# Two-layer hybrid transformer trunk on one core: local attention ahead of latent attention, with nine input projections in pieces beside it, and a conformer convolution over one gapped row

## The chip, the cores and the metric

The kernel runs on one NeuronCore of a Trainium2 chip as one program. The metric is the device time in microseconds (us) of one execution; a profiled execution gives in addition a span, the time between the first and the last recorded instruction. Engines are named as the profile names them: PE (TensorE) multiplies matrices, DVE (VectorE) and ACT (ScalarE) work on tiles element by element, POOL (GpSimd) does some of that too, and SP issues DMAs. Matmul results land in PSUM, everything else lies in SBUF.

## The reference

Two layers run over 256 context tokens and 512 latent tokens of width 1024, in float32. Each layer adds half a SwiGLU feed-forward, then a mixer, then half another feed-forward, each behind a modulated RMS norm and a gate:

```
h += 1/2 * gate1 * SwiGLU_1(mod(norm(h)))
h += gate2 * W_out[ MLA | short conv | windowed GQA + sink | conformer conv ](W_in mod(norm(h)))
h += 1/2 * gate3 * SwiGLU_2(mod(norm(h)))
```

The mixer's four parts read one input projection `W_in` and write into one output projection `W_out`, 256 channels each:

- MLA, here *latent attention*: queries of rank 192, keys and values of rank 128, four heads of 64 + 32 rotary channels; a latent token sees all 768 tokens, a context token the 256 context tokens.
- short conv: `b * dwconv3(c * x)`, three projections of 256 channels.
- windowed GQA, here *local attention*: four query heads, two key heads of 64 channels; a block of 128 latent tokens sees the neighbouring blocks within 128 positions and the context, with a sink in the softmax.
- conformer conv: a gated linear unit, a depthwise convolution over 31 positions with a bias, a layer norm over channels and SiLU. The sequence and the context are convolved apart, each padded with zeros.

Context tokens need no output in the second layer, so that there every query side works on 512 tokens only. The nine modulation vectors of a layer come from products of a conditioning vector with a large weight matrix (`w_mod`).

## The kernel before

Activations lie transposed, channels on partitions and tokens along the row; `TOK` is 768, `SEQ` 512, `CTX` 256. A row holds the 512 latent tokens and then the 256 context tokens. Each matmul runs in a 32-bit format of reduced precision and is made exact enough by splitting both operands into a high and a low part: `split` rounds a tile on ACT (L140) and takes the remainder on DVE (L141), and `mm3` (L169) issues three products. So each weight block of 128 x 512 costs an ACT and a DVE operation before PE can use it (`unit`), and so does each activation tile.

`mixer` (L630) is a Python function that records one layer's mixer in program order; a scheduler then orders each engine's queue by that order and by priorities (`rise`). It records:

1. The norm and the projections of the conformer pair (`T_CFA`, `T_CFG`), then the 31 taps of the conformer convolution on DVE at a low priority (`P_CONV`), so that its operations fill DVE's spare places. `dw_conv` issues a tap as one operation per segment, one over the latent tokens and one over the context.
2. The other 13 projections, each of 8 weight pieces times 3 products over 512 and 256 columns, into three PSUM tiles of 1024 columns that go round (`self.dbl`): latent KV and Q, the window's queries, keys and values, the short convolution's six. Norms, rotations and the first latent queries stand between them.
3. `Latent` units (12 in layer 0, 8 in layer 1): one head and 256 queries each. A unit has two score tiles; each goes through `reduce_max` on DVE (L877), `Exp` with its sum on ACT (L880), `reciprocal` on DVE, normalisation on POOL (L882); then the probabilities are transposed on PE (L602), split by ACT and DVE, and weigh the values on PE (`weigh`, L772 and L773).
4. `Window` units (12, then 8): one block of 128 queries and two heads each, with two PSUM score tiles, the same chain (L825, L833, L837, L840), and the exact sum with the sink.
5. `out` splits each part's result for the output projection; `conformer_norm` goes through its four steps at units that `CN` names.

The loop over units is software-pipelined: the softmax of unit i, the transposes of unit i-1, the values of unit i-2. At the end of a step `spot` lets a generator advance (`fill`), which multiplies one further block of `w_mod` for a later modulation (L186, PSUM tile `mod_ps`, named pmod in the trace; `po`, named pone, collects the weighed values). So a *mod step* is four matmuls with a DMA of its own; the profile records each of them twice.

PSUM is eight banks of 512 columns: pmod, pone and six that the mixer cuts into tiles by `self.psum`. First these are three tiles of 1024, then, for the attention, two of 1024 (`dbls`) and two of 512 (`sgl`).

## Time and profile before

| | us |
|---|---|
| device time, three runs | 2708.47, 2701.59, 2710.09 (median 2708.47) |
| device time of the profiled execution | 2709.64 |
| its span | 2707.9 |
| PE busy | 2635.7 (97%) |
| DVE busy | 2012.7 (74%) |
| ACT busy | 1115.6 (41%) |
| POOL busy | 65.5 (2%) |
| mean granted clock of TensorE | 0.987 of 2.4 GHz |

The span begins with the first recorded instruction and ends with the last, 1.7 us less than the device time. Busy shares are means over the whole span; layer 0's mixer lies between 578 and 892 us, layer 1's between 2040 and some 2300. Lines of the profile are those of the kernel before; after the change the same operations stand some lines further down.

### The profile page before, as it was taken

The numbers are of one execution on the slowest core, as the hardware profiler recorded it, in microseconds if no ns is written. First come the engines' busy times: TensorE is split into PE (matmuls) and PEld (weight loads), VectorE is DVE, ScalarE is ACT, GpSimd is POOL, SyncE is SP. The second block draws the span as 40 slices with busy tenths as digits, with TensorE's granted clock in tenths as the row PEclk, the third lists the DMA queues.
The fourth block names the chain that finished last, engine by engine and source line by source line (L and its number), as shares of the span: only waits on it lengthen the run. The fifth ranks groups of instructions, "written<-read, shape, count | busy, mean of one in ns | idle before, by whom it ended". The sixth has DMA issues, their size and how long they took to land.

```text
span 2707.9 us, 40719 instructions
## 1 busy us (share of the span) xinstructions
PE 2635.7 (97%) x16021; PEld 2446.8 (90%) x16021; DVE 2012.7 (74%) x3940; ACT 1115.6 (41%) x2098; POOL 65.5 (2%) x88
## 2 busy tenths in 40 slices
PE   7999999999989999999999999999999989999998
PEld 5999999988866999999999999999998866889998
DVE  5777666778777486777667867776678786788887
ACT  4323333342376342333224523343244376544444
POOL 0000000000022000000000000000000022000000
PEclk9999999999989999999999999999999989999999
DMA  7323223221123342323223122221122213323322
GB/s 265 115 89 107 86 85 103 94 93 55 55 79 125 98 135 81 115 80 117 75 92 122 55 94 71 64 78 61 63 84 96 71 63 117 118 86 105 99 94 79
DMA packets 78272, 254.68 MB, mean 94 GB/s; under 512 B 8704, under 2 KB 14336, under 8 KB 77824
## 3 DMA queue, kind: packets, MB, share of 16 engines
q1 hardware_dynamic: 78080, 252.08, 28.7%
q8 instruction: 125, 2.05, 0.3%
q14 instruction: 67, 0.55, 0.1%
HBM read 249.95 MB, written 2.10 MB: 93 GB/s over the span
## 4 chain that ended last, share of the span: by engine, by line
PE 91%; DVE 3%; DMA 3%; ACT 2%; issue 1%; POOL 0%; DVEq 0%; SPq 0%; ACTq 0%; POOLq 0%
PE ps L169 74%; PE pone L169 8%; PE pmod L169 3%; PE pmod L186 3%; PE ps L602 1%; DMA mraw<-in_w_mod 1%; PE pone L772 1%; PE pone L773 1%; DMA raw<-in_w_gu 0%; DMA i<-in_w_mod 0%; DMA h<-in_h 0%; DVE r L141 0%; ACT f L140 0%; PE ps L279 0%; ACT f L833 0%
## 5 line engine op out<-in xcount | busy, mean ns | idle before, releaser
L169 PE MATMUL ps<-x,wh 128*128 128x384 f32 (+1 forms) x3064 | 748.8, 329 | 0.0
L169 PEld LDWEIGHTS ps<-x,wh 128*128 128x128 f32 x3064 | 542.8, 188 | 0.1
L169 PE MATMUL ps<-x,wl 128*128 128x384 f32 (+1 forms) x1532 | 505.2, 330 | 0.2 <-ACT x L297 0.2
L140 ACT ACTIVATE wh<-raw 128x512 fp32r<-128x512 f32 x439 | 274.7, 627 | 463.9 <-PE ps L169 316.4
L169 PE MATMUL ps<-t,wh 128*128 128x384 f32 (+2 forms) x1488 | 385.5, 341 | 0.3 <-DVE t L141 0.3
L141 DVE TENSOR_TENSOR wl<-raw,wh 128x512 fp32r<-128x512 f32 x439 | 301.2, 688 | 104.7 <-ACT wh L140 102.1
L169 PE MATMUL ps<-r,wh 128*128 128x512 f32 (+3 forms) x1362 | 339.5, 351 | 0.2 <-DVE r L298 0.2
L303 DVE SCALAR_TENSOR_TENSOR h<-ps,hg,h 128x256 f32<-128x256 f32 (+3 forms) x404 | 186.8, 506 | 187.2 <-PE ps L169 186.5
L169 PEld LDWEIGHTS ps<-x,wl 128*128 128x128 f32 x1532 | 287.8, 188 | 7.9 <-issue 3.7
L169 PEld LDWEIGHTS ps<-t,wh 128*128 128x128 f32 x1488 | 269.2, 188 | 7.1 <-DVE t L141 0.5
L140 ACT ACTIVATE wh<-t 128x512 fp32r<-128x512 f32 x217 | 136.0, 629 | 336.2 <-PE ps L169 200.2
L169 PEld LDWEIGHTS ps<-r,wh 128*128 128x128 f32 (+1 forms) x1362 | 228.7, 189 | 31.8 <-DVE r L298 1.5
L457 DVE TENSOR_TENSOR t<-t,ps 128x384 f32<-128x384 f32 (+1 forms) x422 | 217.2, 520 | 52.1 <-PE ps L169 49.8
L169 PE MATMUL ps<-t,wl 128*128 128x384 f32 (+2 forms) x744 | 253.2, 341 | 1.0 <-ACT t L140 1.0
L140 ACT ACTIVATE t<-t 128x384 fp32r<-128x384 f32 (+2 forms) x247 | 130.4, 536 | 211.9 <-DVE t L451 102.0
L141 DVE TENSOR_TENSOR wl<-t,wh 128x512 fp32r<-128x512 f32 x217 | 149.1, 689 | 90.5 <-ACT wh L140 90.5
L169 PE MATMUL ps<-r,wl 128*128 128x512 f32 (+4 forms) x681 | 212.0, 352 | 0.8 <-ACT r L297 0.8
L169 PE MATMUL ps<-x,t 128*128 128x384 f32 (+1 forms) x1308 | 204.2, 309 | 0.0
L169 PEld LDWEIGHTS ps<-x,t 128*128 128x128 f32 x1308 | 194.1, 188 | 0.0
L169 PE MATMUL ps<-t,t 128*128 128x384 f32 (+2 forms) x948 | 188.8, 345 | 0.0
L169 PEld LDWEIGHTS ps<-t,t 128*128 128x128 f32 x948 | 165.4, 188 | 10.9 <-issue 1.2
L141 DVE TENSOR_TENSOR t<-t,t 128x384 fp32r<-128x384 f32 (+2 forms) x247 | 137.5, 568 | 25.3 <-ACT t L140 24.8
(229 smaller groups left out, 3772.5 us busy)
## 6 DMA issues: line engine op xcount, KB each, us to landing
raw<-in_w_gu SPq DMA_DIRECT2D x160, 512.0 KB, 3.8
mraw<-in_w_mod SPq DMA_DIRECT2D x128, 512.0 KB, 4.4
raw<-in_w_dn SPq DMA_DIRECT2D x88, 512.0 KB, 3.6
raw<-in_w_in SPq DMA_DIRECT2D x34, 512.0 KB, 3.6
raw<-in_w_out SPq DMA_DIRECT2D x20, 512.0 KB, 3.6
i<-in_w_mod SPq DMA_DIRECT2D x32, 256.0 KB, 6.0
raw<-in_w_gu SPq DMA_DIRECT2D x32, 256.0 KB, 3.4
h<-in_h SPq DMA_DIRECT2D x4, 768.0 KB, 6.7
```

Source lines behind the costliest of these rows:

```text
L140: self.nc.scalar.activation(hi, x, AF.Copy)
L141: self.nc.vector.tensor_tensor(out=lo, in0=x, in1=hi.bitcast(F32), op=ALU.subtract)
L169: self.nc.tensor.matmul(ps[:, c:e], a, b[:, c:e], start=start and i == 0, stop=stop and i == 2)
L186: nc.tensor.matmul(ps[32 * j:32 * j + 32, :256], self.sc[:, k, :], r[:, j * 256:(j + 1) * 256], start=k == 0, stop=k == KD - 1)
L303: nc.vector.scalar_tensor_tensor(out=self.h[:, k, s:e], in0=ps[:, s - a:e - a], scalar=gate[:, k, i:i + 1], in1=self.h[:, k, s:e], op0=ALU ...
L457: eng.tensor_tensor(out=out, in0=p, in1=q, op=op)
L602: self.nc.tensor.transpose(out, in_, self.ident)
L772: nc.tensor.matmul(po[:, :256], v, p[1], start=start, stop=False)
L773: nc.tensor.matmul(po[:, :256], v, p[0], start=False, stop=stop)
```

## The change

The recording order of the mixer is turned round, and four things go with it.

- After the conformer pair only the four window projections are recorded, then `window_operands`. The `Window` units come first. The nine other projections become the generator `others`, which yields after each of its 8 weight pieces; the loop over units takes pieces of it three times per step (`more`), so that they spread evenly over the window stage. They go through `slow`, which accumulates into pmod (512 columns) and a further tile `spare` (256 of 512 columns).
- When the window units are recorded, the latent operands are prepared at once (rotary, queries, keys, values), and the `Latent` units follow. Two mod steps are taken in each of their steps (`fill(2)`), none in the window stage; the output splits and the steps of `conformer_norm` stand at fixed units (j = 4 to 9). The query weights are loaded once per layer.
- PSUM: the transposes keep the two tiles of 512 throughout. The other four banks are two tiles of 1024, then for the window stage one tile `quad` of 1536 columns for both heads of a unit and `spare` of 512, then two tiles of 1024 again. A projection of the first stage may also use the pair of 512.
- The conformer convolution's input row has 15 zeros before, between and behind the segments (written by POOL), so that `gap_conv` runs each tap as one operation over 783 columns (512 + 15 + 256) in layer 0, 512 in layer 1. `conformer_norm` reads the segments from their places.

```diff
 class K:
-    WIN, CN = 2, (2, 4, 0, 1)
+    CN = (4, 6, 8, 9)
+    GAP = CF_K // 2
+    WIDE = TOK + 3 * GAP
...
+    def gap_conv(self, y, u, w, bias, n):
+        nc = self.nc
+        mid = CF_K // 2
+        for j in [mid] + [j for j in range(CF_K) if j != mid]:
+            if j == mid:
+                nc.vector.tensor_scalar(out=y[:, :n], in0=u[:, j:j + n], scalar1=w[:, j:j + 1], scalar2=bias, op0=ALU.mult, op1=ALU.add)
+            else:
+                nc.vector.scalar_tensor_tensor(out=y[:, :n], in0=u[:, j:j + n], scalar=w[:, j:j + 1], in1=y[:, :n], op0=ALU.mult, op1=ALU.add)
...
     def mixer(self, l, n, st):
-        dbls = self.psum(st, 2, 1024)
-        third = st.enter_context(ExitStack())
-        self.dbl = dbls + self.psum(third, 1, 1024)
-        sgl = deque()
+        sgl = self.psum(st, 2, 512)
+        cuts = st.enter_context(ExitStack())
+        self.dbl = self.psum(cuts, 2, 1024)
...
             def softmax(w):
...
                 for g in range(2):
-                    ps = self.turn(dbls)
...
-                    nc.vector.reduce_max(mx[:, g:g + 1], ps[:, c0:TOK], axis=AX.X, negate=True)
-                    pss.append(ps)
+                src = [quad[:, c:c + wide] for c in w.c0]
+                for g in range(2):
+                    nc.vector.reduce_max(mx[:, g:g + 1], src[g], axis=AX.X, negate=True)
...
-        units = [Latent(h, tp) for h in range(4) for tp in range(nq // 2)]
-        units += [Window(t, kv) for kv in range(2) for t in range(nq)]
...
+        def slow(t, nt, m=P):
+            rw = self.load(win[l, t], 1024)
+            w = [self.unit(rw[:, :512]), self.unit(rw[:, 512:])]
+            parts = [(0, SEQ, self.mod_ps)] + ([(SEQ, nt, spare)] if nt > SEQ else [])
+            for k in range(KD):
+                wh, wl = w[k // 4]
+                c = slice((k % 4) * P, (k % 4) * P + m)
+                for a, b, ps in parts:
+                    self.mm3(ps[:m, :b - a], (wh[:, c], wl[:, c]), (x[k][0][:, a:b], x[k][1][:, a:b]), k == 0, k == KD - 1)
+                yield
+            return parts
...
+        units = [Window(t, kv) for kv in range(2) for t in range(nq)]
+        units += [Latent(h, tp) for h in range(4) for tp in range(nq // 2)]
+        nw, per = 2 * nq, nq // 2
+        window_operands()
+        while self.open:
+            self.fill()
+        cuts.close()
+        quad, spare = self.psum(cuts, 1, 1536)[0], self.psum(cuts, 1, 512)[0]
...
         for i in range(len(units) + lv):
+            j = i - nw
+            if j == 0:
+                more(1)
...
+                qw, kw = query_weights(), kv_weights()
+                cuts.close()
+                self.dbl = self.psum(cuts, 2, 1024)
+                mraw = self.mraw
+                self.mraw = deque(mraw + deque([self.raw[2], self.raw[3]]))
+                mla_rotary(*qw)
+                mla_queries(0, *qw)
+                mla_keys(0, kw)
...
+                mla_values(kw)
...
-            self.spot()
+            if j >= 0:
+                self.fill(2)
...
-    N_R, N_F = 27, 14
+    N_R, N_F, N_WIDE = 26, 11, 4
```

Two places show how the engines' queues change. The first is PE at a Window unit of layer 0. Its scores (L819, L822, L824 before; L818, L821, L826 after) go into the tiles ps; L172 is `mm3` after the change, r its x operand, wh and wl the weights. Before, a unit's scores stood like this:

```order
L186 MATMUL pmod<-mraw_65,sc 32x256 x3
L819 MATMUL ps_5064<-r_5020,r_5032 128x384
L819 MATMUL ps_5064<-r_5052,r_5032 128x384
L822 MATMUL ps_5064<-masks_r,ident_r 128x128 x2
L824 MATMUL ps_5064<-r_5020,r_5032 128x256
L824 MATMUL ps_5064<-r_5052,r_5032 128x256
L819 MATMUL ps_5060<-r_5020,r_5036 128x384
L819 MATMUL ps_5060<-r_5052,r_5036 128x384
L822 MATMUL ps_5060<-masks_r,ident_r 128x128 x2
...
L186 MATMUL pmod<-mraw_66,sc 32x256
L602 MATMUL ps_6296<-ident,f_4900 128x128
L772 MATMUL pone<-f_4883,r_5056 128x256
```

After the change the like place reads:

```order
L172 MATMUL pmod<-r_4980,wh_73 128x512
L818 MATMUL ps_5705<-r_5036,r_5020 128x384
...
L821 MATMUL ps_5705<-masks_r,ident_r 128x128 x2
L826 MATMUL ps_5705<-r_5036,r_5020 128x256
...
L826 MATMUL ps_5705<-r_5036,r_5024 128x256
...
L818 MATMUL ps_5705<-r_5036,r_5024 128x384
...
L172 MATMUL ps_5709<-r_4980,wl_74 128x256
L172 MATMUL ps_5709<-r_4984,wh_73 128x256
...
L769 MATMUL pone<-f_4879,r_5052 128x256
...
L605 MATMUL ps_5060<-ident,f_4936 128x128
L172 MATMUL pmod<-r_4988,wl_76 128x512
L605 MATMUL ps_5060<-ident,f_4944 128x128
```

Both heads' scores now share one tile (5705), and projection matmuls into pmod and 5709 (`spare`) stand between a unit's scores and the transposes and weighing of the units before it. The second place is DVE at the softmax of a Window unit (L825 maxima, L829, L835, L837 and L838 small operations on the sums sm; L141 and L144 are `split`). Before:

```order
L825 TENSOR_REDUCE sm<-ps_5064 128x1
L829 SCALAR_TENSOR_TENSOR sm<-sm,rc_96 128x2
L835 TENSOR_TENSOR sm<-sm,vec_99 128x2
L141 TENSOR_TENSOR f_4879<-ps_6300,f_4867 128x512
L837 TENSOR_TENSOR sm<-sm 128x2
L838 RECIPROCAL sm<-sm 128x2
L777 TENSOR_TENSOR f_4928<-pone,f_4928 64x256
```

After:

```order
L832 TENSOR_REDUCE sm<-ps_5705 128x1 x2
L630 SCALAR_TENSOR_TENSOR f_4904<-f_4896,vec_99,f_4904 128x783
L835 SCALAR_TENSOR_TENSOR sm<-sm,rc_96 128x2
L630 SCALAR_TENSOR_TENSOR f_4908<-f_4900,vec_99,f_4908 128x783
L841 TENSOR_TENSOR sm<-sm,vec_99 128x2
L630 SCALAR_TENSOR_TENSOR f_4904<-f_4896,vec_99,f_4904 128x783
L630 SCALAR_TENSOR_TENSOR f_4908<-f_4900,vec_99,f_4908 128x783
L630 SCALAR_TENSOR_TENSOR f_4904<-f_4896,vec_99,f_4904 128x783
L843 TENSOR_TENSOR sm<-sm 128x2
L630 SCALAR_TENSOR_TENSOR f_4908<-f_4900,vec_99,f_4908 128x783
L844 RECIPROCAL sm<-sm 128x2
```

The taps of the conformer convolution (L630), which before ran to their end under the projections, now stand between the softmax's operations of the first Window units; in layer 0, 29 taps come ahead of the window stage and 31 in it, beside the two that start the sums.

## Rows read from the trace of the kernel before

**Rows 1.** The page's first part: busy us (share of the span) and instructions per engine.

```profile
PE 2635.7 (97%) x16021; PEld 2446.8 (90%) x16021; DVE 2012.7 (74%) x3940; ACT 1115.6 (41%) x2098; POOL 65.5 (2%) x88
```

**Rows 2.** The page's fourth part: the chain that ended last, shares by engine.

```profile
PE 91%; DVE 3%; DMA 3%; ACT 2%; issue 1%; POOL 0%; DVEq 0%; SPq 0%; ACTq 0%; POOLq 0%
```

**Rows 3.** Busy time by stretch: us, each engine's busy us (instructions), granted clock, DMA.

```profile
600.00:640.00 40.00, 40.00 (x243) 35.18 (x242) 36.38 (x67) 14.79 (x23) 0.00 (x0) 1.00 0.26 80
640.00:660.00 20.00, 20.00 (x102) 17.09 (x101) 15.68 (x31) 6.87 (x11) 0.00 (x0) 0.83 0.09 27
...
752.00:835.00 83.00, 74.00 (x477) 58.04 (x476) 66.14 (x145) 58.75 (x114) 21.82 (x26) 0.89 0.28 89
835.00:892.00 57.00, 51.13 (x383) 37.77 (x383) 41.42 (x122) 37.73 (x104) 14.52 (x23) 0.97 0.38 121
...
2180.00:2243.00 63.00, 51.89 (x318) 40.47 (x317) 53.12 (x103) 45.75 (x82) 16.70 (x16) 0.92 0.20 65
2243.00:2300.00 57.00, 53.97 (x397) 41.15 (x396) 39.04 (x101) 37.80 (x92) 11.78 (x16) 0.97 0.33 105
...
1040.00:1060.00 20.00, 20.00 (x116) 20.00 (x115) 16.05 (x33) 6.54 (x13) 0.00 (x0) 1.00 0.34 123
```

**Rows 4.** PE's timeline near 780 us: start, length, operation; xN are merged neighbours.

```profile
779.59 1.03 PE L602 MATMUL ps<-ident,f 128*128 128x128 f32 x8
780.55 0.64 PE L186 MATMUL pmod<-mraw,sc 128*32 128x256 f32 x8
```

**Rows 5.** PE's groups by form, 740 to 892: count | busy, mean ns | idle before.

```profile
L602 PE MATMUL ps<-ident,f 128*128 128x128 f32 x202 | 37.2, 297 | 2.2 <-POOL f L840 0.9 <-DVE sm L829 0.8
L772 PE MATMUL pone<-f,r 128*128 128x256 f32 x92 | 27.4, 318 | 3.8 <-DVE f L777 3.6
L169 PE MATMUL ps<-r,r 96*128 96x512 f32 x48 | 22.6, 488 | 2.5 <-DVE r L141 1.7 <-ACT f L880 0.8
L186 PE MATMUL pmod<-mraw,sc 128*32 128x256 f32 x202 | 22.5, 405 | 4.0 <-DMA mraw<-in_w_mod 4.0
L169 PE MATMUL ps<-r,r 96*128 96x256 f32 x72 | 20.5, 319 | 1.9 <-ACT f L880 1.8
```

**Rows 6.** The same view of PE, 2160 to 2300: its first and last group.

```profile
L602 PE MATMUL ps<-ident,f 128*128 128x128 f32 x174 | 31.9, 289 | 1.8 <-POOL f L882 1.2 <-DVE f L141 0.4
...
L169 PE MATMUL ps<-r,wl 128*128 128x256 f32 x2 | 0.6, 278 | 0.0
```

**Rows 7.** DVE's groups by form: conformer taps in 580 to 740, L743 in 740 to 892.

```profile
L620 DVE SCALAR_TENSOR_TENSOR f<-f,vec,f 128x511 f32<-128x511 f32 x8 | 6.0, 750 | 0.0
L620 DVE SCALAR_TENSOR_TENSOR f<-f,vec,f 128x255 f32<-128x255 f32 x8 | 3.9, 483 | 0.0
...
L743 DVE SCALAR_TENSOR_TENSOR f<-ps,f 128x768 f32<-128x768 f32 x2 | 1.8, 953 | 0.9 <-PE ps L261 0.9
```

**Rows 8.** DVE's groups by form in 740 to 892: Window units' maxima and sums.

```profile
L825 DVE TENSOR_REDUCE sm<-ps 128x1 f32<-128x640 f32 x8 | 6.4, 815 | 0.2
...
L837 DVE TENSOR_TENSOR sm<-sm 128x2 f32<-128x2 f32 x12 | 1.9, 160 | 6.7 <-ACT sm L836 6.6
```

**Rows 9.** Timelines of POOL, then DVE, 815 to 822 us: start, length, operation.

```profile
815.95 1.69 POOL L882 TENSOR_SCALAR f<-f,sm 128x768 f32<-128x768 f32 x1 [5.66 <-DVE sm L878]
817.88 0.91 POOL L882 TENSOR_SCALAR f<-f,sm 128x768 f32<-128x768 f32 x1 [0.24 <-DVE sm L881]
...
815.91 0.94 DVE L141 TENSOR_TENSOR r<-f,r 128x768 fp32r<-128x768 f32 x1
...
818.31 0.49 DVE L878 TENSOR_TENSOR sm<-sm,rq 128x1 f32<-128x1 f32 x1
...
820.45 0.14 DVE L878 TENSOR_TENSOR sm<-sm,rq 128x1 f32<-128x1 f32 x1
820.51 0.69 DVE L141 TENSOR_TENSOR wl<-raw,wh 128x512 fp32r<-128x512 f32 x1
```

**Rows 10.** ACT's timeline near 603 us: a table switch.

```profile
603.25 1.28 ACT L674 ACT_TABLE_LOAD   x1
```

More of the change, by code (lines that the diff above doesn't have):

```diff
@@ L657, in proj_parts @@
                     norm(a, b)
-                for w, ps in zip(ws, pss):
+                for w, whole in zip(ws, pss):
                     for k in range(KD):
@@ L669, in mixer @@
         dd = []
         us = []
+        gap = self.GAP
+        places = [(a, b, a + i * gap) for i, (a, b) in enumerate(segs)]
         for i in range(2):
+            u = self.wide.popleft()
+            for c in [0] + [p + gap + b - a for a, b, p in places]:
+                nc.gpsimd.memset(u[:, c:c + gap], 0.0)
             pa, pg = proj_parts([T_CFA + i, T_CFG + i], ((0, SEQ), (SEQ, TOK)) if i == 0 else [(0, n)])
-            u = self.S()
-            nc.scalar.activation(u[:, :n], pg[:, :n], AF.Sigmoid)
@@ L675, in mixer @@
-            nc.vector.tensor_tensor(out=u[:, :n], in0=pa[:, :n], in1=u[:, :n], op=ALU.mult)
+            for a, b, p in places:
+                v = u[:, p + gap:p + gap + b - a]
+                for c, e, ps in pieces(a, b, pg):
+                    nc.scalar.activation(v[:, c - a:e - a], ps, AF.Sigmoid)
+                for c, e, ps in pieces(a, b, pa):
+                    nc.vector.tensor_tensor(out=v[:, c - a:e - a], in0=ps, in1=v[:, c - a:e - a], op=ALU.mult)
             us.append(u)
-        def conformer_conv():
+        with self.rise(self.P_CONV):
@@ L679, in conformer_conv @@
             for i in range(2):
-                y = self.S()
-                yield from self.dw_conv(y, us[i], self.vcol(l, "wcf", i * CF_K, CF_K), CF_K, self.vcol(l, "bcf", i), segs)
+                y = self.wide.popleft()
+                a, b, p = places[-1]
+                self.gap_conv(y, us[i], self.vcol(l, "wcf", i * CF_K, CF_K), self.vcol(l, "bcf", i), p + b - a)
                 dd.append(y)
-        with self.rise(self.P_CONV):
-            for _ in conformer_conv():
-                pass
@@ new lines, in softmax, with near @@
+                for g, c, cc in ((0, w.c0[0], SEQ), (1, 1024, TOK)):
+                    q = wqs[kv][g]
+                    parts = (q[:, ts_], wks[kv][0]), (q[:, ts_], wks[kv][1])
+                    def near():
+                        if b1 > b0:
+                            kc = slice(b0 * P, b1 * P)
+                            for i, (a, b) in enumerate(parts):
+                                nc.tensor.matmul(quad[:, c:c + w.n], a, b[:, kc], start=i == 0, stop=False)
+                            edges = ([(0, c)] if t > 0 else []) + ([(1, c + w.n - P)] if t < 3 else [])
+                            for i, (mi, e) in enumerate(edges):
+                                nc.tensor.matmul(quad[:, e:e + P], self.ident_r, self.masks[:, mi, :], start=False, stop=i == len(edges) - 1)
+                    if g == 0:
+                        near()
+                    for i, (a, b) in enumerate(parts):
+                        nc.tensor.matmul(quad[:, cc:cc + CTX], a, b[:, SEQ:], start=i == 0, stop=i == 1)
+                    if g == 1:
+                        near()
@@ L1027, in mixer @@
-        for hi, lo in x:
-            self.give(hi, lo)
-        third.close()
-        sgl.extend(self.psum(st, 2, 512))
-        self.dbl = dbls
-        kw = kv_weights()
-        mla_keys(0, kw)
-        self.give(qb)
-        mla_values(kw)
-        units[0].softmax()
-        qw = query_weights()
-        out(2, ob[0])
-        out(3, ob[1])
-        lt, lv = self.LAGS
-        cn = conformer_norm()
-        for i in range(len(units) + lv):
-            if i == self.PAIR[per]:
+        def slow(t, nt, m=P):
[9 more added lines that the diff above has]
+            return parts
@@ new lines, in mixer, with more @@
+        units = [Window(t, kv) for kv in range(2) for t in range(nq)]
[6 more added lines that the diff above has]
+        quad, spare = self.psum(cuts, 1, 1536)[0], self.psum(cuts, 1, 512)[0]
+        lt, lv = self.LAGS
+        cn, rest, done, total = conformer_norm(), others(), 0, 9 * KD
+        def more(share):
+            nonlocal done
+            while done < min(total, round(total * share)):
+                next(rest, None)
+                done += 1
@@ new lines, in mixer @@
+        for i in range(len(units) + lv):
+            j = i - nw
+            if j == 0:
+                more(1)
+                for _ in rest:
+                    pass
+                qw, kw = query_weights(), kv_weights()
[6 more added lines that the diff above has]
+                mla_keys(0, kw)
+                self.give(lat["kr"])
+                mla_values(kw)
+            if j == self.PAIR[per]:
@@ L1052, in mixer @@
             turned = units[i - lt].turned() if 0 <= i - lt < len(units) else iter(())
-            for _ in range(3):
+            for u in range(3):
                 next(values, None)
                 next(turned, None)
+                if j < 0:
+                    more((3 * i + u + 1) / (3 * nw))
             for g in (values, turned):
```

249 lines of the change are left out of this document (131 added, 118 removed).

## The prediction

> **What bounds the kernel now.** I read the page's first part before anything else: PE is busy 97% of the span, DVE 74%, ACT 41% [rows 1]. The chain that ended last agrees, with 91% of it on PE [rows 2]. So the time is PE's work plus what PE loses, and the change can only move the second: the order has 15,351 matmuls on PE both before and after. Where PE loses is seen in the busy times by stretch [rows 3]. In the projections (600 to 640 us) PE never pauses. In the attention it does: Latent units (752 to 835) and Window units (835 to 892) of layer 0, then the same two in layer 1 (2180 to 2243, 2243 to 2300), each after a short hand-over from the last projections. Idle time is only part of the loss there, since the records of a starved PE overlap with gaps that the pipeline hides, and the granted clock falls to 0.89 to 0.97. So I price the work itself.
>
> Prices: 116 matmuls of 384 columns fill 20.00 us back to back, 0.172 us each, 0.45 us per 1000 columns [rows 3]; eight transposes start at 779.59 and end their turn at 780.55, 0.12 us each; eight records of a mod step take 0.64 us [rows 4]. With these, 740 to 892 holds 202 transposes (24 us), 92 weighing matmuls of 256 columns and as many partners (21), 48 and 72 score matmuls of 512 and 256 (19), 202 mod records (16) and 18 smaller groups (28): 108 us of work in 152 us, 44 lost [rows 5]. In 2160 to 2300 the same prices over 22 groups (first and last shown) give 106 of 140, 34 lost [rows 6]. The projection stretches ahead of them lose some 18 more by these prices; the largest piece shown is 640 to 660, with the clock at 0.83 [rows 3]. Lost in both mixers: 96; with the transposes and the mod records at 0.11 and 0.07 (the pauses before the next row left out of both) 105. I take 100.
>
> **The change, part by part.** The order divides each new mixer into three stages, and I sum each engine's instructions in a stage by the durations of the same form in this trace (on DVE less an estimated 0.055 us each, since its records overlap: the operation of 0.14 at 820.45 is followed at 820.51 [rows 9]).
>
> *Conformer convolution.* A tap now costs an operation of 511 elements and one of 255: 0.750 + 0.483 us [rows 7]. After, it is one of 783. The nearest row is a 768-wide one at 0.953 [rows 7], hence 0.97; net of overlap 0.92 to 0.95 against 1.12. 62 taps in layer 0 save some 12 us of DVE; in layer 1 there is one segment in both, and nothing is saved. Ten 128x15 memsets on POOL have no row; POOL is busy 2% [rows 1], and what they clear is wanted only after the first projections, 20 us later, so I count nothing; at most they are ten of the 0.91 us that POOL takes for 768 elements [rows 9], 9 us, hidden by the same projections.
>
> *Stage one* (norm, conformer and window projections, start of the convolution): PE 77 us, DVE 78.5 in layer 0 (29 taps 27, 32 norm operations 18, 19 weight splits 12, rotations and operands 21). Two engines level: DVE reached 91% in 600 to 640 with PE full [rows 3]; at 93% this stage takes 84. Layer 1: PE 64, DVE 62, hence 66.
>
> *Stage two* (Window units with nine projections between): PE 103 (projections 9 x 24 matmul products of 768 columns, 75; the units' own scores, transposes and weighing 28). DVE 90: 31 taps 29, 33 splits of 512 elements 21 (0.69 each [rows 9]), 24 maxima 14 (the widest 0.815 [rows 8]), small softmax operations 5, joins 5, short convolution and latent preparation 16. The gap that PE has today under each unit's softmax is filled: between one unit's scores and the next unit's stand 21 to 43 projection matmuls in layer 0 and 13 to 37 in layer 1, of which the PE rows of the order show one piece.
>
> What this stage adds is contention. Convolution and weight splits read two SBUF operands, and the probabilities are normalised on POOL meanwhile. The trace has that meeting: a split from SBUF starts at 815.91, POOL's normalisation at 815.95 takes 1.69 us instead of the 0.91 of its neighbour at 817.88, and a tiny DVE operation started under that one takes 0.49 instead of the 0.14 of its like at 820.45 [rows 9]. I charge 0.35 for each of the 24 and 16 normalisations in this stage: 8 us on DVE in layer 0, 5 in layer 1. Lower bound nothing (they miss each other); upper bound the whole normalisation, 0.66 on average, 16 and 11.
>
> The Trainium skill, "SBUF — State Buffer", section "SBUF: two separate sides", states that a DVE operation with two SBUF inputs and a GpSimd operation that reads SBUF share one exclusive lock, held for the whole instruction. The rows above agree with it. By that rule with every normalisation met in full, the sum below would be some 15 us worse, about 2697.
>
> So DVE has 98 us, PE 103: I take 107 for the stage, which also holds some 4 us for the first units, whose scores follow each other with only 4 to 5 us of priced PE work between, while one score tile must first be read by two maxima (0.815 each [rows 8]) and two exponentials. Layer 1: PE 76, DVE 70 + 5, hence 82.
>
> *Stage three* (latent preparation, Latent units, conformer norm, output splits, 28 mod steps): no projection is left as cover. DVE 82 (32 splits 20, maxima 17, operand splits and outputs of 0.9 us 17, joins, reciprocals and the rest 28), ACT 81, PE 74. ACT's sum has five table switches among the exponentials, at 1.28 us each [rows 10], 6 us; eight more in the whole kernel, 10 us of an engine busy 41%. DVE was used 80% in today's Latent stretch (66.14 of 83) and 73% in the Window stretch (41.42 of 57) [rows 3]. I take 78%, since ACT is as full here: 105. Layer 1: DVE 66.5, hence 82 at 81%. Hand-over from stage two (the last projection's square sums, a table switch, root, reciprocal, then the queries): 2 us in each layer, covered in part by mod steps.
>
> *DMA.* The query weights are loaded once per layer rather than twice, six DMAs less on SP. Two spare weight buffers take mod blocks in stage three, so the wait for those loads should shrink. DMA's share in these stretches is 0.20 to 0.38 [rows 3]: I count nothing, a microsecond either way.
>
> *Sum.* Layer 0: 84 + 107 + 105 + 2 = 298 against 254 of PE work, 44 lost. Layer 1: 66 + 82 + 82 + 2 = 232 against 204 (203 to 205), 28 to 29 lost. 73 lost instead of 100: 27 us gained. The profiled execution took 2709.6, 1.2 above the median of the runs. **2709.6 − 27 = 2682.6; I predict 2682.** Own range: the loss before between 96 and 105, contention between 0 and 27 on DVE where 9 and 6 of slack hide a part, stage three between 73% and 84%: 2665 to 2700.
>
> **Rivals.**
> A, *more is gained.* Stage three runs as close as the projections do, at 91% DVE: 90 and 73 instead of 105 and 82, 24 us; stage two at PE's own 103 and 77, 9 us more: 2649 to 2665. For it: twelve fewer exposed Window units and more mod steps as cover. Against it: DVE, ACT and PE are all at 74 to 82 in that stage, and each unit is a chain through all three.
>
> B, *the gain is given back in stage three.* Today the Latent units have the first queries and the output splits spread around them; after, preparation, conformer norm, four outputs and the table switches all meet there. At the Window stretch's 73% [rows 3] it takes 112 and 91, 16 us more, and 10 more if the first Window units stall on the one score tile by 2.5 us in two gaps of each layer: 2708, no difference.
>
> C, *slower: DVE waits in order.* The convolution's operations stand between the softmax's small ones, so whenever a small one waits, work that could run is shut in behind it. Today DVE waits 6.7 us over 12 units for the sum of exponentials [rows 8], 0.56 each, with nothing urgent behind. If waits of the score maxima and sums come to 3 us per unit over 20 units, 60 us less the 9 and 7 of slack between DVE and the stage's length make stage two 44 longer: 2726. It is slower than before by over 8 us (0.3%, which is about what a measurement of this kernel can tell) from 2.6 us per unit on. Against it: at least 13 projection matmuls per unit keep PE running, and 2.6 is nearly five times today's wait.
>
> **How the numbers follow.** Forecast 0.50; A 0.20; B 0.16; C 0.14. 2682 is the likeliest. Faster by over 0.3% (below 2700) is forecast and A, 0.70; within 0.3% B, 0.16; slower C, 0.14. The range runs from the bottom of A, 2648, to 2716: it leaves out C and some 0.05 of A.
>
> **What would show it.** Right: PE 100% busy or nearly in the stretch of Window units with a clock of 1.00, a pause in PE of under 2 us at the first units; convolution operations at 0.95 to 1.0 us, some at 1.3 to 1.7 under a normalisation; stage three still with PE idle and a clock under 1, ended by DVE and ACT, in 100 to 110 us and 78 to 88. Wrong: idle PE in stage two ended by exponentials or maxima (C), stage three at 112 or longer (B) or near 90 (A), DVE operations of the convolution mostly lengthened (the upper bound of contention).

## The result and the profile after

| | before | after |
|---|---|---|
| device time, median of 12 runs each | 2707.25 us | 2692.51 us |
| ratio, with its 95% interval | | 0.9944 [0.9932, 0.9956] |
| span of the profiled execution | 2707.9 us | 2691.5 us |

The change makes the kernel 0.56% faster, about 15 us; 27 were forecast. Timed again beside the last experiments, the same kernel gave 0.9961 [0.9946, 0.9977], so a difference of two or three thousandths between two kernels of different sets is not one to build on. The time of an execution goes with its mean granted clock: the changed kernel's twelve run from 2686.54 us at 0.993 to 2698.97 at 0.986. At one clock, 0.989, nine executions of the kernel before on record take 2700.95 to 2705.25 us and nine of the changed kernel 2691.86 to 2696.72, so about 11 of the 15 us remain where the clock is equal.

The page's first part of the changed kernel, to be held against [rows 1], and its chain that ended last against [rows 2]:

```profile
PE 2622.2 (97%) x16021; PEld 2443.5 (91%) x16021; DVE 2000.5 (74%) x3882; ACT 1124.7 (42%) x2115; POOL 73.7 (3%) x98
```

```profile
PE 64%; DVE 6%; ACT 2%; DMA 1%; issue 1%; POOL 0%; DVEq 0%; ACTq 0%; POOLq 0%
```

PE is still busy 97%, with 13.5 us less of it; DVE lost 12 us. The chain's shares add to under 75%, so they say less than before; what stands in them is PE first, as in [rows 2], and now the convolution (L630) among DVE's lines.

Where the 16.4 us of the two spans went is read from marks that both programs have, the first matmul of each norm: the mixer of layer 0 with its output projection takes 379.3 us instead of 385.3, that of layer 1 288.9 instead of 297.4, the feed-forward ahead of layer 1's mixer 526.5 instead of 530.0, and the rest 1.6 more. The gain is thus in the mixers. Which layer gains more is not settled: in a second trace of the changed kernel the mixers take 381.4 and 292.6. The next rows are the two mixers, before and then after (columns as in [rows 3]):

```profile
577.70:963.00 385.30, 364.93 (x2260) 307.85 (x2259) 287.99 (x599) 188.24 (x367) 36.34 (x48) 0.95 0.27 88
2039.70:2337.10 297.40, 279.56 (x1631) 222.83 (x1629) 233.52 (x441) 159.60 (x303) 28.48 (x32) 0.97 0.29 92
```

```profile
578.80:958.10 379.30, 358.68 (x2292) 306.17 (x2291) 280.83 (x543) 194.88 (x383) 41.03 (x54) 0.96 0.28 94
2030.80:2319.80 289.00, 273.29 (x1632) 219.76 (x1630) 230.83 (x439) 162.10 (x306) 31.95 (x36) 0.98 0.29 93
```

PE's idle time hardly fell, from 38.2 to 36.3 us; its busy time fell by 12.5 for nearly the same matmuls, which stand closer together and run at a higher granted clock. The clock's part of that in these two traces is an estimate: lengths times what the clock lacks to 1.00 come to 28 us before and 21 after.

The busy times by stretch answer to [rows 3]; the stretches are the stages of the changed kernel: the projections, the first three Window units, the rest of them, the last projections, the hand-over, stage three, then Window units, hand-over and stage three of layer 1.

```profile
600.00:660.30 60.30, 59.65 (x352) 52.10 (x351) 57.84 (x82) 24.43 (x38) 0.00 (x0) 1.00 0.22 70
660.30:685.40 25.10, 21.91 (x129) 19.26 (x129) 22.55 (x38) 11.33 (x26) 3.92 (x4) 0.93 0.14 39
685.40:742.00 56.60, 55.60 (x357) 49.46 (x356) 53.86 (x111) 24.90 (x66) 13.59 (x14) 1.00 0.07 23
742.00:775.60 33.60, 32.87 (x213) 28.27 (x212) 17.77 (x45) 20.36 (x48) 3.92 (x6) 1.00 0.21 64
775.60:801.20 25.60, 19.98 (x143) 14.12 (x141) 17.20 (x29) 19.17 (x30) 0.00 (x0) 0.87 0.47 165
801.20:891.30 90.10, 81.23 (x568) 63.70 (x568) 65.01 (x151) 63.58 (x118) 19.26 (x24) 0.91 0.34 114
...
2100.70:2188.10 87.40, 82.06 (x473) 68.89 (x473) 74.06 (x147) 44.22 (x102) 15.56 (x16) 1.00 0.16 50
2188.10:2209.70 21.60, 18.77 (x134) 12.85 (x132) 15.39 (x27) 16.77 (x28) 0.00 (x0) 0.84 0.41 141
2209.70:2274.60 64.90, 59.86 (x435) 46.93 (x431) 51.87 (x113) 46.23 (x88) 16.15 (x16) 0.97 0.33 111
```

From 685 to 742 PE runs almost without a pause at a clock of 1.00, where before the Window units had PE busy 51.13 of 57 [rows 3]. The loss has not gone, it sits elsewhere. The priced loss of a stretch is its length less PE's work at fixed prices. With the prices of the prediction (of its two for transposes and for mod records I take 0.11 and 0.08), PE loses in layer 0: 4.4 us in stage one, 6.5 in the first three units, 6.9 in the rest of stage two, 11.6 in the 25.6 us of the hand-over and 24.2 in the 90.1 of stage three, 54 in all. In layer 1 it is 5.8, 11.5, 8.3 and 12.2, 38 in all. The same prices on the trace of before give 60 and 47.

Two places on PE's timeline show it. Columns: start, length, operation, and in brackets the idle time before it with what ended it.

```profile
665.34 0.40 PE L172 MATMUL ps<-r,wh 128*128 128x256 f32 x2
667.76 0.62 PE L818 MATMUL ps<-r,r 128*128 128x384 f32 x2 [2.02 <-ACT f L839]
```

The second unit's scores (L818) wait 2.02 us until the exponentials of the first (L839) have read the one score tile; this is the stall that the prediction gave to the first units.

```profile
779.72 0.38 PE L1074 MATMUL ps<-ones,f 128*128 128x2 f32 x2
...
780.97 0.59 PE L1074 MATMUL ps<-ones,f 128*128 128x2 f32 x2
...
795.51 0.39 PE L172 MATMUL ps<-wh,r 128*128 128x256 f32 x1 [1.73 <-DVE r L144]
...
801.17 1.27 PE L172 MATMUL ps<-r,r 96*128 96x512 f32 x3 [2.60 <-DVE r L144]
```

This is the hand-over. L1074 and L1075 are the two halves of the sums of squares for the latent queries, together 12 matmuls of two columns with 24 records. Two records take 0.38 at 779.72 and 0.59 at 780.97. The next view cuts the hand-over in three (columns as in [rows 3]):

```profile
775.60:781.00 5.40, 5.20 (x35) 4.29 (x33) 3.52 (x6) 4.89 (x8) 0.00 (x0) 0.99 0.01 3
781.00:787.00 6.00, 6.00 (x40) 3.74 (x40) 2.17 (x5) 1.60 (x3) 0.00 (x0) 0.50 0.31 82
787.00:801.20 14.20, 8.79 (x71) 6.09 (x70) 11.51 (x19) 12.69 (x19) 0.00 (x0) 0.97 0.72 262
```

From 781 to 787 the granted clock is 0.50, the lower level of 1.2 GHz, with PE busy throughout: it fell while PE did these narrow matmuls, and the rest of them, four mod steps and the first matmuls of the queries run at half speed. Then PE is idle for 5 of 14 us; the longest single waits are for splits on DVE, 1.73 us of the values and 2.60 of the first Latent scores. Part of the 11.6 us is no wait: the narrow matmuls' 24 records, some 0.155 us apart at the full clock, take nearly 4 us themselves, in the kernel before as well, and the prices count some 1 us for them.

### The profile page after: what moved, and what is told of

It is laid out like the page before. It is cut to its first block, busy times and chain, and to the rows that moved or that the text cites. A ratio compares the mean times of both kernels' runs of the same rounds, so it can differ in the third digit from the quotient of the medians.

```text
span 2691.5 us, 40599 instructions
## 1 busy us (share of the span) xinstructions
PE 2622.2 (97%) x16021; PEld 2443.5 (91%) x16021; DVE 2000.5 (74%) x3882; ACT 1124.7 (42%) x2115; POOL 73.7 (3%) x98
## 3 DMA queue, kind: packets, MB, share of 16 engines
q1 hardware_dynamic: 77472, 251.30, 28.4%
## 4 chain that ended last, share of the span: by engine, by line
PE 64%; DVE 6%; ACT 2%; DMA 1%; issue 1%; POOL 0%; DVEq 0%; ACTq 0%; POOLq 0%
PE ps L172 48%; PE pone L172 5%; PE pmod L172 5%; PE pmod L189 2%; DVE f L630 2%; PE ps L605 1%; DVE wl L144 1%; DMA raw<-in_w_gu 1%; PE pone L769 1%; PE pone L770 1%; DVE sm L832 0%; DVE f L144 0%; ACT r L143 0%; ACT wh L143 0%; ACT f L143 0%
## 5 line engine op out<-in xcount | busy, mean ns | idle before, releaser
L172 PE MATMUL ps<-x,wh 128*128 128x384 f32 (+1 forms) x3064 | 748.0, 329 | 0.0
L172 PEld LDWEIGHTS ps<-x,wh 128*128 128x128 f32 x3064 | 542.5, 188 | 0.2
L172 PE MATMUL ps<-x,wl 128*128 128x384 f32 (+1 forms) x1532 | 504.9, 330 | 0.0
L172 PE MATMUL ps<-t,wh 128*128 128x384 f32 (+2 forms) x1488 | 385.7, 341 | 0.3 <-DVE t L144 0.3
L144 DVE TENSOR_TENSOR wl<-raw,wh 128x512 fp32r<-128x512 f32 x437 | 300.8, 691 | 104.6 <-ACT wh L143 102.3
L172 PEld LDWEIGHTS ps<-x,wl 128*128 128x128 f32 x1532 | 287.6, 188 | 7.5 <-issue 3.7
L172 PEld LDWEIGHTS ps<-t,wh 128*128 128x128 f32 x1488 | 269.2, 188 | 7.2 <-DVE t L144 0.5
L172 PE MATMUL ps<-r,wh 128*128 128x512 f32 (+3 forms) x1074 | 262.5, 336 | 0.4 <-DVE r L301 0.2
L172 PE MATMUL ps<-t,wl 128*128 128x384 f32 (+2 forms) x744 | 253.0, 341 | 0.9 <-ACT t L143 0.9
L144 DVE TENSOR_TENSOR wl<-t,wh 128x512 fp32r<-128x512 f32 x217 | 149.1, 689 | 92.1 <-ACT wh L143 92.0
L172 PE MATMUL ps<-x,t 128*128 128x384 f32 (+1 forms) x1308 | 204.2, 309 | 0.0
L172 PEld LDWEIGHTS ps<-r,wh 128*128 128x128 f32 (+1 forms) x1074 | 180.9, 187 | 21.6 <-DVE r L301 1.3
L172 PEld LDWEIGHTS ps<-x,t 128*128 128x128 f32 x1308 | 194.1, 188 | 0.0
L172 PE MATMUL ps<-t,t 128*128 128x384 f32 (+2 forms) x948 | 188.4, 345 | 0.0
L172 PEld LDWEIGHTS ps<-t,t 128*128 128x128 f32 x948 | 165.8, 188 | 9.7
L172 PE MATMUL ps<-r,wl 128*128 128x256 f32 (+3 forms) x537 | 171.2, 338 | 2.9 <-ACT r L300 1.8
L144 DVE TENSOR_TENSOR t<-t,t 128x384 fp32r<-128x384 f32 (+2 forms) x247 | 137.6, 569 | 24.7 <-ACT t L143 24.3
```

Source lines behind the costliest of these rows:

```text
L144: self.nc.vector.tensor_tensor(out=lo, in0=x, in1=hi.bitcast(F32), op=ALU.subtract)
L172: self.nc.tensor.matmul(ps[:, c:e], a, b[:, c:e], start=start and i == 0, stop=stop and i == 2)
```

## The experiments

Each was run five rounds beside the kernel before; ratios are to that kernel, with a 95% interval. Eleven are changes to one of the two kernels or sums of such, one is the changed kernel again.

**Without the cover (no_beside).** The six short-convolution projections ahead of the Window units, the three latent ones behind them:

```diff
+        more(6 / 9)
         for i in range(len(units) + lv):
...
-                if j < 0:
-                    more((3 * i + u + 1) / (3 * nw))
```

> The changed kernel with no projection beside the Window units: the six short-convolution projections are recorded ahead of them, the three latent ones behind them. Theory one (the projections are the cover that makes the gain): the Window units lose what they lost before, 15 to 20 us in layer 0 and 10 to 12 in layer 1, so 2715 to 2725, at or above the kernel before. Rival (order and cover matter little, the gain is from the convolution or the PSUM cut): within 5 us of 2692.

Measured: 2711.49 us, 1.0019 [1.0007, 1.0030], slower than the kernel before, a little below the range of theory one and far from the rival. In the stretches below (700 to 745 holds Window units, 745 to 806 the last of them, the latent projections and the preparation) PE pauses again:

```profile
700.00:745.00 45.00, 41.05 (x279) 36.12 (x278) 36.53 (x93) 26.39 (x73) 10.02 (x15) 1.00 0.10 31
745.00:806.00 61.00, 48.91 (x316) 36.84 (x315) 33.85 (x73) 35.44 (x75) 4.69 (x8) 0.97 0.29 90
...
2180.00:2226.00 46.00, 41.32 (x250) 30.82 (x249) 26.40 (x52) 29.04 (x54) 3.52 (x4) 0.85 0.30 99
```

```profile
PE ps L172 <- DVE r L144: 3.6, 1, 3.6
PE ps L605 <- DVE f L144: 2.1, 3, 1.0
...
PE pone L769 <- DVE f L774: 1.4, 2, 1.2
PE pmod L172 <- DVE f L1038: 1.4, 2, 1.0
```

PE now waits for splits, joins and the gate products, each a little. By the prices the two mixers lose 67 and 43 us, 18 more than with the cover. The mixers' own rows:

```profile
575.60:968.00 392.40, 363.99 (x2293) 307.28 (x2291) 282.57 (x543) 191.99 (x380) 36.97 (x54) 0.96 0.28 91
2041.10:2335.10 294.00, 275.25 (x1632) 220.72 (x1630) 229.86 (x439) 163.66 (x306) 32.56 (x36) 0.98 0.29 92
```

At the same granted clocks as with the cover, PE is idle 10.8 us longer and busy 7.3 longer. That is the whole gain of the change, and a little more: the projections beside the Window units make it, and the order without them costs time. One thing besides the place differs from the kernel before: the projections still go through `slow` and its one tile pmod, for which PE waits 3.6 us from 661 to 806, some 2 more than in the changed kernel. So a small part of the 18 may belong to that tile; the order without cover and with the three tiles that go round was not run.

**The convolution in two operations (two_ops), and its new form alone in the kernel before (before_gap).**

```diff
-                nc.vector.scalar_tensor_tensor(out=y[:, :n], in0=u[:, j:j + n], ...
+            for a, b in ((0, SEQ), (SEQ + self.GAP, n)) if n > SEQ else ((0, n),):
+                    nc.vector.scalar_tensor_tensor(out=y[:, a:b], in0=u[:, j + a:j + b], ...
```

> The changed kernel with each tap of the conformer convolution again as two operations (512 and 256 columns) in layer 0; all else as changed. DVE is 96% busy in the first stage of layer 0 (600 to 660 us), so its added 11 to 13 us should show. Theory one (DVE is level with PE in stages one and two): 5 to 12 us more than the changed kernel's 2692.5, about 2697 to 2705, with stage one of layer 0 several us longer. Rival (PE hides it, DVE has room later in the window stage): 2692 to 2695.

> The kernel before with the gapped convolution alone (one operation per tap, zero gaps written by POOL, ten full tiles of 768 instead of fourteen). Theory one (the order makes the gain; the projection stretch before had PE full and DVE at 91%): 0 to 4 us less than before, 2703 to 2708. Rival (the saved DVE time makes the gain): 10 us or more less, 2697 or below.

before_gap also trades four of its fourteen tiles of 768 for the four wide ones. Measured: 0.9939 [0.9926, 0.9953] for the first, no different from the changed kernel; 0.9995 [0.9986, 1.0004] for the second, no different from the kernel before. In the first, DVE is fuller, and PE does not mind. The rows are its stretches and its taps by form (count | busy, mean ns):

```profile
600.00:659.00 59.00, 58.43 (x342) 50.73 (x342) 56.67 (x103) 24.02 (x38) 0.00 (x0) 1.00 0.23 72
659.00:742.00 83.00, 77.70 (x498) 69.57 (x499) 80.57 (x181) 36.35 (x92) 17.29 (x18) 1.00 0.09 28
```

```profile
L631 DVE SCALAR_TENSOR_TENSOR f<-f,vec,f 128x512 f32<-128x512 f32 x56 | 43.2, 772 | 0.1
L631 DVE SCALAR_TENSOR_TENSOR f<-f,vec,f 128x256 f32<-128x256 f32 x56 | 27.5, 491 | 0.1
```

With DVE busy 80.57 of 83 us from 659 to 742, the Window units took no longer. So the taps are hidden, also at 97% of DVE: the scheduler gives them the lowest priority, so that they yield to the softmax, and after 742 DVE has room (17.77 of 33.6 us above). My expectation for two_ops, 5 to 12 us, was wrong; the rival held.

**The hand-over (latent_first).** The three latent projections stand ahead of the last short-convolution projection, so that sums, root, rotation and splits lie under it:

```diff
             for i in range(2):
...
-                for a, b, ps in (yield from slow(T_SC + i, n)):
-                    nc.vector.tensor_tensor(out=cv[:, a:b], in0=ps[:, :b - a], in1=cv[:, a:b], op=ALU.mult)
                 ob.append(cv)
+                if i == 0:
+                    yield from gate(0)
...
             lat["kr"] = qb
+            yield from gate(1)
+            for t in x:
+                self.give(*t)
```

> The changed kernel with the three latent projections ahead of the last short-convolution projection, so that the square sums, the root, the rotation and the splits of the latent queries lie under that projection. In the changed kernel 775.6 to 795.5 us of layer 0 hold the hand-over: 24 matmuls of two columns, a clock that falls to half, and waits for splits. Theory one (the hand-over loses 7 to 9 us per layer where 2 were forecast): 3 to 6 us per layer are won, 2681 to 2687. Rival (the same chain only waits elsewhere, or stage three is bound by ACT and DVE whenever it starts): 2690 to 2694.

Measured: 2683.12 us, 0.9917 [0.9900, 0.9933], within theory one. That is some 7 us under the changed kernel, and 6.5 under two_ops, which ran in the same set; both intervals touch this one, so alone it does not settle the gain (combo_act below does, together with act_norm). Its hand-over (two stretches, then the waits of PE in them), and beneath, the waits in the changed kernel's:

```profile
756.00:776.00 20.00, 19.11 (x103) 16.49 (x102) 8.91 (x22) 10.82 (x22) 2.11 (x4) 0.83 0.18 54
776.00:795.10 19.10, 16.19 (x135) 12.22 (x133) 16.47 (x27) 15.58 (x25) 0.00 (x0) 1.00 0.48 161
```

```profile
PE pmod L189 <- DMA raw<-in_w_mod: 1.0, 1, 1.0
...
PE ps L172 <- DVE r L144: 0.9, 1, 0.9
```

```profile
PE ps L172 <- DVE r L144: 4.8, 3, 2.6
PE pmod L189 <- DMA raw<-in_w_mod: 0.7, 1, 0.7
```

The waits for splits fall from 4.8 to 0.9 us; the changed kernel's second trace has 5.3. In layer 0 the clock still falls, now under the last projection (0.83 in 756 to 776) instead of in the preparation, which runs at 1.00; so there the gain is in the waits, not in a fall avoided. Layer 1's mixer ran at 1.00 throughout, 0.98 in the changed kernel (289 us, so some 6 us as an estimate); whether the order did that or chance is not shown. By the prices, up to the next norm, layers 0 and 1 lose 51 and 34 us where the changed kernel lost 55 and 40, so the hand-over looks like a loss of its own, and one that order can mend in part.

**The meeting of POOL with DVE (act_norm).** The Window units' normalisation on ACT:

```diff
-                    nc.gpsimd.tensor_scalar(out=w.prs[g][:, :wide], in0=w.prs[g][:, :wide], scalar1=sm[:, g:g + 1], scalar2=1.0,
-                                            op0=ALU.mult, op1=ALU.mult)
+                    nc.scalar.activation(w.prs[g][:, :wide], w.prs[g][:, :wide], AF.Copy, scale=sm[:, g:g + 1])
```

> The changed kernel with the Window units' probabilities normalised on ACT instead of POOL. In the changed kernel the trace shows tap and split operations on DVE lengthened by 0.25 to 0.63 us under a normalisation, some 4 us in all over both layers' window stages, normalisations of 512 columns lengthened from 0.69 to 1.1 to 1.5, and PE waiting 3.5 us for POOL. Theory one (this meeting costs the window stages time): 2 to 6 us less, 2686 to 2690, with normal tap lengths. Rival (PE hides it; ACT, at 50 to 60% there, gets 24 and 16 more operations of some 0.7 us in each exponential's way): no change or up to 5 us more, 2692 to 2697.

Measured: 2689.16 us, 0.9929 [0.9916, 0.9943]; its interval overlaps both of the changed kernel's, so in time this is not decided. The meeting itself is seen. First POOL and DVE of the changed kernel, then its taps and normalisations of 512 columns from 660 to 742 and the taps of act_norm:

```profile
692.64 2.88 POOL L846 TENSOR_SCALAR f<-f,sm 128x512 f32<-128x512 f32 x2 [5.31 <-DVE sm L844]
...
693.59 1.38 DVE L630 SCALAR_TENSOR_TENSOR f<-f,vec,f 128x783 f32<-128x783 f32 x1
```

```profile
L630 DVE SCALAR_TENSOR_TENSOR f<-f,vec,f 128x783 f32<-128x783 f32 x33 | 34.9, 1068 | 0.3
```

```profile
L846 POOL TENSOR_SCALAR f<-f,sm 128x512 f32<-128x512 f32 x6 | 7.1, 1190 | 102.4 <-DVE sm L844 93.0 <-ACT wh L143 9.4
```

```profile
L630 DVE SCALAR_TENSOR_TENSOR f<-f,vec,f 128x783 f32<-128x783 f32 x33 | 33.7, 1027 | 0.3
```

Two normalisations of 512 columns take 2.88 us (0.69 each where they run alone), and a tap started under them 1.38. But over 33 taps the mean falls only from 1068 to 1027 ns, 1.4 us in all: three taps take 1.34, 1.38 and 1.57 us, the other thirty 1.01 to 1.10. POOL bears more of the meeting than DVE: six normalisations of 512 columns come to 1.19 us each, 3 us in all above 0.69.

**The first units (lean_front).** More pieces beside the first Window units, by `more(((3 * i + u + 1) / (3 * nw)) ** 0.8)`:

> The changed kernel with the projection pieces leaning to the first Window units: the share done after a step is the step's share to the power 0.8, so the first unit has 10 pieces beside it instead of 6. In the changed kernel PE waits 2.0 us for the exponentials of the first unit (665 to 668), and its clock is 0.89 there. Theory one (PE has too little between the first units' scores, since one score tile serves both heads): 2 to 5 us less, nearly all in 660 to 690, so 2687 to 2691. Rival (what is lost there is only moved to the last units, which then have fewer pieces): 2691 to 2694.

Measured: 2687.75 us, 0.9932 [0.9917, 0.9948], in theory one's range but not distinct from the changed kernel. PE's wait for the first exponentials stands as it was:

```profile
PE ps L818 <- ACT f L839: 2.0, 1, 2.0
```

In its order the same 23 projection matmuls stand between the first two units' scores as in the changed kernel; the scheduler put the added pieces behind them (33 instead of 21 before the third unit). So the edit did not do at that place what it was meant to, and the number is no support for theory one. What the first units' stall is worth stays open.

**More mod steps in stage three (fill3)**, `self.fill(3)` for `self.fill(2)`:

> The changed kernel with three mod steps instead of two in each step of stage three (mod steps are taken from the feed-forward that follows). Theory one (PE loses some 25 us in stage three for want of work that depends on nothing there): part of the added steps, 14 of 0.6 us in layer 0, run in time that is lost now; 3 to 8 us less, 2684 to 2689. Rival (PE takes its queue in order, so a mod step stands in the way of the unit's chain, or waits for its weight load): no change or more, 2691 to 2698.

Measured: 2694.81 us, 0.9951 [0.9937, 0.9965], no gain, as the rival had it. Stage three of layer 0:

```profile
796.00:894.20 98.20, 86.73 (x650) 65.26 (x651) 66.76 (x153) 66.80 (x120) 18.93 (x24) 0.90 0.46 159
```

It has 9.4 us more priced work up to the next norm and takes 11.4 longer; layer 1 has less left to do and is shorter by as much. PE loses time in stage three, yet work put into its queue there costs its full length. A likely reason is that the units' chain through ACT and DVE is what PE waits for, and that a mod step ahead of a unit's matmuls delays the chain. It is not shown: PE's wait for exponentials (L887) there is 7.0 us, 6.3 in the changed kernel.

**The conformer norm earlier (cn_early)**, `CN = (0, 1, 2, 3)`:

> The changed kernel with the four steps of the conformer norm at the first four steps of stage three (j = 0 to 3) instead of 4, 6, 8 and 9. DVE is busy only 51 to 56% at 742 to 786 and 74% at 786 to 800 of layer 0, ACT 60% and 82%. Theory one (stage three loses most where norm, outputs and units meet late): 2 to 5 us less, 2687 to 2690. Rival (the hand-over is the tight place, and its table switches for the root and the sigmoid-like function then lie ahead of the first exponentials): 2 to 6 us more, 2694 to 2699.

Measured: 2696.62 us, 0.9962 [0.9948, 0.9975], no better, as the rival had it; in layer 0 the priced loss from the first Latent scores to the next norm rises from 25.5 to 28.4. The place of the norm in the change is as good.

**Rotary copies on POOL (pool_copy)**, `nc.gpsimd.tensor_copy` for the ACT copies of L939 and L951, on the changed kernel:

> The changed kernel with the six and four copies of rotary rows into each layer's latent queries and keys (0.84 us each on ACT, all in the hand-over and stage three) moved from ACT to POOL, which is idle in the hand-over. Theory one (ACT bounds hand-over and stage three: PE waits most for exponentials there): 6 and 5 us of ACT freed, 2 to 5 us less than the changed kernel, 2687 to 2690. Rival (DVE bounds them, or PE's own order; POOL, which holds up DVE's operations from SBUF, then makes it worse): 2692 to 2698.

Measured: 2699.77 us, 0.9979 [0.9968, 0.9990], above both ranges; not distinct from the changed kernel's 0.9961 beside it (2696.49), but not better either. The copies by form on ACT (changed kernel) and POOL (this one), and PE's wait in its hand-over:

```profile
L939 ACT ACTIVATE r<-r 32x768 fp32r<-32x768 f32 x4 | 3.4, 841 | 0.1
```

```profile
L939 POOL CAST r<-r 32x768 fp32r<-32x768 f32 x4 | 5.3, 1318 | 3.8 <-ACT r L143 3.6
```

```profile
PE ps L172 <- DVE r L144: 5.6, 3, 3.0
```

A copy takes 1.32 us on POOL instead of 0.84, and PE's wait for splits on DVE is 5.6 us, where the changed kernel's two traces have 4.8 and 5.3. So the wait neither shrinks nor clearly grows. Relieving ACT in the hand-over does not help; DVE is named as what comes last there, before and after.

**The base again, and two sums.** The changed kernel once more, then latent_first with act_norm (combo_act), then these with lean_front (combo_both).

> The changed kernel itself, timed beside the three others of this set, as their base. Both theories: 0.9944 of the kernel before, within 0.993 to 0.9956; 2690 to 2695, and window stages and hand-overs of the same length to within 2 us.

> The changed kernel with the latent projections ahead of the last short-convolution projection (2683 when alone) and the Window units' normalisation on ACT (2689 when alone). Theory one (hand-over and the meeting of POOL with DVE are separate losses): the gains add, 2677 to 2681. Rival (both only fill the same few idle places of PE, or the gain of the second was chance): 2682 to 2685.

> The same as the one before with the projection pieces leaning to the first Window units as well (share to the power 0.8, 2688 when alone). Theory one (the first units' stall is a loss of its own): 2674 to 2679. Rival (PE's wait of 2.0 us at the first unit stood as it was with the lean alone, so that its gain was not there): as the one before, within 2 us.

Measured: 0.9961 [0.9946, 0.9977], 0.9920 [0.9905, 0.9935] and 0.9898 [0.9881, 0.9914]. The first, at 2696.49 us, lies above the range expected, and its layer 1 is 4.6 us longer up to the first Latent scores, where 2 were allowed. The second is apart from the first in the same set: latent_first and act_norm together gain 0.4%. What act_norm adds to latent_first's 0.9917 of another set is not settled. With the lean it is 2678.26 us, 28 us under the kernel before and the best version found; the page's first part:

```profile
PE 2619.0 (98%) x16021; PEld 2445.5 (91%) x16021; DVE 1996.9 (75%) x3882; ACT 1150.6 (43%) x2155; POOL 36.4 (1%) x58
```

Its interval touches that of combo_act, so what the lean adds is not settled.

## Why the forecast was right in kind and off in size

*The base.* I took 100 us lost before; by the same records, cut at the mixers' first norm and first output matmul, it is 107. The gain is 107 less 92, 15.6 us of the 16.4 between the spans. So the loss left was forecast 19 us too low (73) and the base 7 too low, and the second error hides part of the first by luck. Of the 19, stage two has 15, stage three with the hand-over 3; stage one is 3 better than forecast in layer 0 and 4 worse in layer 1.

*Stage one*: 84 and 66 forecast, 81.6 and 69.9 measured. Right in layer 0, short in layer 1.

*Conformer convolution.* The tap came to 1.03 us undisturbed, 0.95 from start to start, as forecast with overlap; but the 12 us of DVE that it saves are worth nothing that could be measured (two_ops, before_gap). The stage sums that took DVE as level with PE ("at 93% this stage takes 84") priced a saving that PE covers.

*Stage two*: 107 and 82 forecast, 115.3 and 87.4 measured. **This is the term that failed**: its cover was right (no_beside: without it all of the gain is gone), and so was PE's work, 102 us against 103. The loss was put at 4 us and is 13: 6.5 in the first three units (2.0 of it waiting for the single score tile, 1.2 for POOL, and a clock of 0.93), 6.9 in the rest. In layer 1 it was put at 6 and is 11.5. The 8 us charged to contention were too much and on the wrong engine: DVE's longer taps are 1.4 us, three taps of 33, and POOL's normalisations lengthen instead.

*Hand-over*: 2 us forecast, 11.6 and 8.3 lost. I counted the chain of sums, root and splits, and not that all latent preparation waits in one line behind the narrow matmuls. Nor did I count the clock's fall during them, but in layer 0 that is no new price: it falls at the same sums in the kernel before and in latent_first. The Latent units needed this preparation before, too, but it lay under short-convolution projections. latent_first puts part of it back there, and PE's waits for splits shrink.

*Stage three*: hand-over and stage together were 107 and 84, and measured 115.7 and 86.5. In layer 0 some 6 of the 9 us are work, 80 us on PE where I had 74. They are not mod steps beyond the forecast: the trace has 224 records of them there, the 28 that I had counted. Which part of the sum was short stays open. The loss of both together, 36 us, is 3 above what 107 less 74 meant; only its places were wrong, more in the hand-over and 24.2 in the units. From 801 to 891 DVE is used 72% (65.01 of 90.1), as in the Window stretch before [rows 3], not 78. More mod steps do not fill it (fill3), and moving six and four copies off ACT does not ease it (pool_copy).

*DMA*: PE's waits for mod blocks did shrink, from 4.0 us [rows 5] and 5.8 in the attention stretches before to 1.9 and 2.7 after, of which 0.7 and 2.7 lie in the hand-overs, where DMA is busy 0.47 and 0.41. That is 5 us of waits where I counted nothing, a microsecond either way. Whether it is time won is not shown: no run changes it alone.

*The rivals.* C did not occur: in 685 to 742, with the taps between the softmax's operations and DVE busy 95%, PE lost 4 us. A did not: stage three runs at 72% of DVE, not 91%. B named a right place: hand-over and stage three hold 36 of layer 0's 54 us of loss and 20 of layer 1's 38. By my own sign for B, 112 us or longer, layer 0 is B's case (115.7, where 2 of hand-over were counted apart) and layer 1 is not (86.5 against 91); the time came out between B and the forecast, 10 us from the one and 16 from the other. The Trainium skill's rule of the lock shared by DVE and GpSimd ("SBUF — State Buffer", section "SBUF: two separate sides") agrees with the operations that meet, as the 1.38 us tap and the two normalisations of 2.88 us show. The price of 15 us that I worked out with it is not borne out: few DVE operations meet a normalisation, and PE has other work.

## What to carry to other kernels

Work that only PE needs is the cover for chains through DVE and ACT: spread in pieces between units, it let PE run through a softmax stage that had idled it, and taking it away cost 0.6 to 0.75%. Cover is moved, not made: ask which chain it stood over before, because that one is bare now, and let the next chain's preparation end under the last piece. A saving on an engine whose work has low priority and yields was worth nothing here, even at 97% of that engine: ask first whether it ends a wait of the bottleneck.

## What the runs showed of the hardware

PE's clock fell during matmuls of two columns. In the changed kernel the pairs of records of L1074 and L1075 go from 0.38 to 0.59 us at 781 while PE does nothing else, and the clock is 0.50 up to 787. In the kernel before the same sums stand at 647 to 652, inside the stretch with 0.83 [rows 3], with the same rise from 0.38 to 0.58 us, and latent_first has 0.83 where they stand there:

```profile
649.76 0.38 PE L709 MATMUL pone<-ones,f 128*128 128x2 f32 x2
650.07 0.58 PE L710 MATMUL pone<-ones,f 64*128 64x2 f32 x2
```

In layer 0, with 12 such matmuls, the fall begins during them or within about a microsecond behind them in every trace kept here. Layer 1 has eight, and there it does not always come: the clock falls at 2194 in the changed kernel, just behind them, and in latent_first, where they stand at 2176 to 2179, it stays at 1.00:

```profile
2174.00:2190.00 16.00, 15.80 (x90) 13.29 (x89) 11.71 (x23) 13.09 (x23) 0.49 (x1) 1.00 0.10 33
```

The matmuls that run at half speed behind such sums are a price that the sums' own 4.6 us (778.5 to 783.0) don't show. A copy of 32 x 768 takes POOL 1.32 us and ACT 0.84. The same kernel in two sets differed by 0.0017 of the time, and by 7.6 us between two profiled spans, of which 4.6 lie in layer 1's mixer up to the first Latent scores.
